# The three changes of stage of a two-layer transformer step: written order on every engine, and twelve modulation chunks in three bursts

## The chip, the core and the metric

One core of a Trainium2 chip runs the whole step. The metric is the device time of one execution in microseconds (us), the median of several runs; smaller is better. TensorE (PE) multiplies, VectorE (DVE) and ScalarE (ACT) do elementwise work, GpSimd (POOL) takes powers, and SyncE's queue (SP) issues nearly all transfers (DMA).

## What is computed

Two rows of tokens, stream 0 (128 context tokens) and stream 1 (128 latent tokens), go through two layers of width 2048 with the same weights, in fp32:

```
sh_a, sc_a, gt_a, sh_m, sc_m, gt_m = silu(c) @ w_ada + b_ada      # modulation, per layer and per stream
h = rms_norm(x, g1) * (1 + sc_a) + sh_a                           # pre-norm
x = x + gt_a * rms_norm(attention(h @ w_in) @ w_out, g2)          # attention half
h = rms_norm(x, g3) * (1 + sc_m) + sh_m
x = x + gt_m * rms_norm(relu(h @ w_up)**2 @ w_down, g4)           # MLP half, width 8192
```

## The kernel before

**Products.** A weight chunk is 1 MB: 128 rows of 2048 numbers, which hold two k-tiles (128 inputs each) for 1024 outputs. `issue` (line 1003) loads chunks on SP's queue, in one order for the whole kernel, into five buffers (`NRAW`); a buffer is filled again when its chunk is used. `split_to` (1012) splits each half chunk (one k-tile) into a high part `wh` (an ACT copy, 1020) and a low part `wl` (a DVE subtraction, 1021), three pairs deep (`NW`). `Group.run` (350) multiplies: per k-tile, stream and 512 outputs three products, `xh*wh`, `xh*wl` and `xl*wh` (365 to 367), so 24 products a chunk. The left sides lie transposed and split in `XT[0..3]`, four k-tiles each.

**A change of stage** lies between the last product of one half layer and the first product of the next. There are three: attention to MLP in layer 0, MLP of layer 0 to attention of layer 1, and attention to MLP in layer 1. At each, for both streams, the last outputs are squared for the norm (864 or 937) and multiplied by the gate rows (865 or 938). `residual` (316) then adds them to x (326) and squares the new x (330); `rstd` (104) takes the root on POOL (107). `make_xt` (261) scales x by it (269 for stream 0 on DVE, 271 for stream 1 on ACT), transposes blocks of 128 columns on PE (`tr`, line 120), applies scale and shift (280 on DVE, 282 on ACT), and splits into XT (287 on ACT, 288 on DVE).

**Modulation.** A column block of 512 of `w_ada` is either four chunks on PE (`ada_mm`, 139: eight products of 32 columns of the array each; then a copy `pt`, 151, transposes and small sums in `ada_post`, 158), or four chunks of the transposed weights on DVE (`dv_mul`, 206: two passes over the chunk, line 212, with `sB`, silu of c, as the other factor). `PE_BLOCKS` and `DV_BLOCKS` say which block goes where. PE chunks are woven between the product chunks, the DVE chunks of layer 1 run under the MLP of layer 0. At each change of stage PE has eight chunks: four from the chunk buffers (`TAIL`, or the first four of `last`) and four that `ahead` (722) loaded early into the then idle XT tiles. They all run right behind the last product of the old stage.

**Order.** A planner places each engine's instructions by the order in which they are written and by when its own model has them ready; it may move one ahead of others. `behind` (109) pins single ones. Transfers are moved too: at the second change the reload of `sB` (204) and the store of x (309) are written some chunks into the new stage.

Of the kernel before, what the change touches and what calls it, by code (L numbers as in the profile page):

```python
# [19 lines left out]
L = 2  # L20
D = 2048
# [9 lines left out]
TAIL = 4  # L31
# [6 lines left out]
DV_BLOCKS = [G_M, M_A + M_M[:4] + G_A[:3] + G_M]  # L38
PE_BLOCKS = [M_A[2:] + G_A + M_M, M_M[4:] + G_A[3:]]
# [28 lines left out]
def trunk(ctx: ExitStack, tc: tile.TileContext, I, O):  # L68
    nc = tc.nc
    pe, act, dve, pool = nc.tensor, nc.scalar, nc.vector, nc.gpsimd  # L70
# [45 lines left out]

    mark = {"pt": None, "res": None, "xt": None}

# [20 lines left out]
    def ada_mm(l, blks, t, kq, raw, half=None):  # L139

        w = 512 if half is None else 256
        if (t, kq) == (0, 0):
            ada_live["ps"] = ps.tile([P, 512], F32, tag="ada", bufs=1, name="ada")
        pa = ada_live["ps"]
        end = t == len(blks) - 1 and kq == 3
        for g in range(4):
            pe.matmul(pa[32 * g:32 * g + 32, 0:w], sT[:, 4 * kq + g, 2 - 2 * t:34 - 2 * t], raw[:, g * w:(g + 1) * w],  # L147
                      start=((t, kq) == (0, 0)), stop=end, tile_position=(0, 32 * g))
        if end:
            pt = sb([P, 512], "pt")  # L150
            mark["pt"] = act.activation(pt[:, 0:w], pa[:, 0:w], AF.Copy)
            fast.append(ada_post(l, blks, pt, 0 if half is None else 2 * half, w // P))
# [104 lines left out]
    def new_xt():  # L257
        for f in range(4):
            XT[f] = sb([P, 4, 2, 256], f"XT{f}", dt=F32R)

    def make_xt(l, w, f, j0=0, j1=4):

        scl, sh = mods[l][2 * w], mods[l][2 * w + 1]
        c, cn = slice(512 * f + P * j0, 512 * f + P * j1), slice(P * j0, P * j1)
        for s in range(2):
            r = xr[s][:, s:s + 1]
            xn, t = nt[0][:, 2 * s], nt[0][:, 2 * s + 1]
            if s == 0:
                dve.tensor_scalar(xn[:, cn], x[s][:, c], r, None, ALU.mult)
            else:  # L270
                act.activation(xn[:, cn], x[s][:, c], AF.Copy, scale=r)
            m = psm()
            for j in range(j0, j1):
                tr(m[:, j * P:(j + 1) * P], xn[:, j * P:(j + 1) * P])
            step = 2 if f == 0 else 4
            for j in range(j0, j1):
                k = 4 * f + j
                jc = slice(j * P, (j + 1) * P)
                if s == 0:
                    dve.tensor_scalar(t[:, jc], m[:, jc], scl[:, k, s:s + 1], sh[:, k, s:s + 1], ALU.mult, ALU.add)  # L280
                else:
                    act.activation(t[:, jc], m[:, jc], AF.Identity, bias=sh[:, k, s:s + 1], scale=scl[:, k, s:s + 1])
                if (j + 1) % step == 0:
                    i = j + 1 - step
                    tv = t[:, i * P:(j + 1) * P].rearrange("p (j q) -> p j q", j=step)
                    hi = XT[f][:, i:j + 1, 0, s * P:(s + 1) * P]
                    act.activation(hi, tv, AF.Copy)  # L287
                    lo = dve.tensor_tensor(XT[f][:, i:j + 1, 1, s * P:(s + 1) * P], tv, hi.bitcast(F32), ALU.subtract)
        mark["xt"] = lo
# [26 lines left out]
    def residual(rows, ss, last, s):  # L316

        if not last and s == 0:
            nt[0] = sb([P, 4, 512], "big", 5)
        r = st2()  # L320
        dve.tensor_reduce(r[:, 0:1], ss[:, s, :], AX.X, ALU.add)
        rstd(r[:, 0:1], r[:, 0:1], D, 1)
        ss2 = st2()
        for n in range(4):
            c = slice(n * 512, (n + 1) * 512)
            u = dve.scalar_tensor_tensor(x[s][:, c], rows[s][:, c], r[:, 0:1], x[s][:, c], ALU.mult, ALU.add)  # L326
            if last:
                nc.sync.dma_start(O["yp" if s == 0 else "ys"][:, c], x[s][:, c])
            else:
                q = act.activation(rows[s][:, c], x[s][:, c], AF.Square, accum_out=ss2[:, n:n + 1])  # L330
                if s == 1 and n == 2:
                    behind(q, mark["pt"])
        if s == 0:
            mark["res"] = u
        if not last:
            xr[s] = st2()
            dve.tensor_reduce(xr[s][:, s:s + 1], ss2[:, 0:4], AX.X, ALU.add)
            rstd(xr[s][:, s:s + 1], xr[s][:, s:s + 1], D, 1)


    class Group:


        def __init__(self, ntile, nk, lhs, done, seg=None):
# [3 lines left out]
            self.q = self.cnt = 0  # L348

        def run(self, steps):  # L350

            if self.acc is None:
                self.acc = [[ps.tile([P, 512], F32, tag="acc", bufs=NACC, name="acc") for _ in range(self.n)]
                            for _ in range(2)]
            q, i0 = self.q, self.cnt - self.segs[self.q]
            seg = self.segs[q + 1] - self.segs[q]
            end = i0 + len(steps) == seg
            for s in range(2):
                for n in range(self.n):
                    a = self.acc[s][n]  # L360
                    for i, (kt, wh, wl) in enumerate(steps):
                        first, last = i0 + i == 0, i0 + i == seg - 1
                        c = slice(n * 512, (n + 1) * 512)
                        xh, xl = self.lhs(kt, s, 0), self.lhs(kt, s, 1)
                        pe.matmul(a, xh, wh[:, c], start=first, stop=False)  # L365
                        pe.matmul(a, xh, wl[:, c], start=False, stop=False)  # L366
                        pe.matmul(a, xl, wh[:, c], start=False, stop=last)  # L367
                    if end:
                        self.done(s, n, a, q)
# [352 lines left out]
    def ahead(ada):  # L722
# [9 lines left out]
        def use():  # L732
            for t, it in zip(held, ada):
                ada_mm(*it[2], t)
                step_list(fast, 1)
# [28 lines left out]
    for l in range(L):  # L764
# [34 lines left out]
        call(new_xt)  # L799
        call(begin)  # L800
# [34 lines left out]
        else:  # L835
            for f in range(4):
                call(lambda f=f: make_xt(1, 0, f))
            cG[0].insert(3, ("call", store_x))
            cG[0].insert(1, ("call", reload_sb))
# [19 lines left out]
        def wout_done(nh, S=S, l=l):  # L859
            def f(s, n, a, _):  # L860
# [4 lines left out]
                dve.tensor_tensor(S["rows"][s][:, c], S["rows"][s][:, c], a, ALU.mult)  # L865
                if (nt, s) == (1, 1):
                    load_x()
                if (nt, s) == (3, 0):
                    residual(S["rows"], ssA[0], False, 0)
# [5 lines left out]
        for nh in range(2):  # L875
            rest += tchunks(I["w_out"][l], 8 * nh, 8, Group(2, KT, o_lhs(), wout_done(nh)), ko, need)
# [7 lines left out]
        weave(rest[cut:], fill[nf:], tail=TAIL)  # L884

        def after_attn(S=S, l=l, use=use):
            mark["tail"] = mark["pt"]
            use()
            drain_dv()
            drain_fast()  # L890
            new_xt()
            mark["pt"] = mark["tail"]
            residual(S["rows"], ssA[0], False, 1)

        call(after_attn)
        for f in range(4):
            call(lambda f=f, l=l: make_xt(l, 1, f))
# [25 lines left out]
        def down_done(q, nh, M=M, l=l):  # L923
            def f(s, n, a, _):
# [9 lines left out]
                if q == 3:  # L934
# [3 lines left out]
                    dve.tensor_tensor(rw[:, c], rw[:, c], sB[s][:, c], ALU.mult)  # L938
                    if (nt, s) == (3, 0):
                        residual(M["rows"], ssA[1], l == L - 1, 0)  # L940
            return f

        if l + 1 < L:
            last = ada_items(1, G_A[3:] + M_M[4:5])
            load, use = ahead(last[4:])
        rest = []
        for q in range(4):
            for g in range(2 * q, 2 * q + 2):
                rest += tchunks(I["w_up"][l], 8 * g, 8, Group(2, KT, xl, up_done(g)), k2)
            for nh in range(2):  # L950
                al = lambda kt, s, p, M=M, q=q: M["a"][4 * q + kt // 4][:, kt % 4, p, s * P:(s + 1) * P]
                rest += tchunks(I["w_down"][l], 16 * q + 8 * nh, 8, Group(2, KT, al, down_done(q, nh)), k2)
            if q == 3 and l + 1 < L:
                rest.insert(-8, ("call", load))
        if l + 1 < L:
            rest.insert(1, ("call", load_sb))
            g, m = dv_items(0, G_M), dv_items(1, M_A + M_M[:4])
            dv = [x for i in range(16) for x in m[3 * i:3 * i + 3] + g[i:i + 1]]
            weave(rest[:4], [])
            weave(rest[4:115], [], dv)  # L960
            call(lambda: (drain_dv(), drain_fast()))
            items.append(rest[115])
            call(lambda l=l: load_gates(l, 1, sB, slice(0, D)))
            call(lambda l=l: layer_consts(l + 1))
            items.extend(rest[116:])
            items.extend(last[:4])
        else:
            weave(rest[:2], [])
            weave(rest[2:100], [], dv_items(1, G_M))
            call(lambda: (drain_dv(), drain_fast()))  # L970
            items.append(rest[100])
            call(lambda l=l: load_gates(l, 1, sB, slice(0, D)))
            items.extend(rest[101:])

        def after_mlp(M=M, l=l, use=use):
            if l + 1 < L:
                mark["tail"] = mark["pt"]
                use()
                mark["pt"] = mark["tail"]
            drain_fast()  # L980
            residual(M["rows"], ssA[1], l == L - 1, 1)

        call(after_mlp)
# [10 lines left out]
    chunks = [it for it in items if it[0] != "call"]  # L994
# [17 lines left out]
    def split_to(k):  # L1012
        while state["split"] <= min(k, len(subs) - 1):
            i, j = subs[state["split"]]
            if i not in raws:
                return
            r = raws[i][:, j * 1024:(j + 1) * 1024]
# [3 lines left out]
            behind(dve.tensor_tensor(wl, r, wh.bitcast(F32), ALU.subtract), mark["res"])  # L1021
# [128 lines left out]
```

## Time and profile before

| | us |
|---|---|
| runs: median of 3 (lowest, highest) | 2297.96 (2296.06, 2302.87) |
| the profiled execution, its own time | 2295.36 |
| its span in the profile | 2293.3 |
| PE busy | 2223.2 (97%) |
| DVE busy | 1592.6 (69%) |
| ACT busy | 1072.2 (47%) |
| mean granted TensorE clock | 0.993 of full |

How to read it: the span runs from the first to the last instruction. The line of an instruction is that of `kernel.py`; all transposes have line 120. A wait is written "engine line <- what released it". The granted clock is a share of 2.4 GHz. PE is busy nearly all of the time, so the time ends with PE's work and the gaps in it.

### The profile page before, as it was taken

The numbers are of one execution on the slowest core, as the hardware profiler recorded it, in microseconds if no ns is written. First come the engines' busy times: TensorE is split into PE (matmuls) and PEld (weight loads), VectorE is DVE, ScalarE is ACT, GpSimd is POOL, SyncE is SP. The second block draws the span as 40 slices with busy tenths as digits, with TensorE's granted clock in tenths as the row PEclk, the third lists the DMA queues.
The fourth block names the chain that finished last, engine by engine and source line by source line (L and its number), as shares of the span: only waits on it lengthen the run. The fifth ranks groups of instructions, "written<-read, shape, count | busy, mean of one in ns | idle before, by whom it ended". The sixth has DMA issues, their size and how long they took to land.

```text
span 2293.3 us, 26818 instructions
## 1 busy us (share of the span) xinstructions
PE 2223.2 (97%) x10460; PEld 1746.8 (76%) x10460; DVE 1592.6 (69%) x1967; ACT 1072.2 (47%) x1483; POOL 23.3 (1%) x30
## 2 busy tenths in 40 slices
PE   6999999999999999999999999999999999999997
PEld 3667666678888888888867777876888888888886
DVE  2566745499899998999668787548566566565445
ACT  4334444365445434434446455545544543443443
POOL 0000000000000000000000000000000000000000
PEclk9999999999999999999999999999999999999999
DMA  8888787978788887788868666766566566556652
GB/s 335 313 336 333 300 313 309 397 295 298 295 310 300 298 302 294 282 295 313 317 225 299 237 248 218 270 232 230 205 230 233 203 220 236 205 211 223 221 189 93
DMA packets 94539, 611.40 MB, mean 267 GB/s; under 512 B 14026, under 2 KB 16458, under 8 KB 22730
## 3 DMA queue, kind: packets, MB, share of 16 engines
q1 hardware_dynamic: 93836, 609.21, 72.1%
q8 instruction: 82, 1.34, 0.2%
q10 hardware_dynamic: 576, 0.48, 0.1%
q14 instruction: 45, 0.37, 0.0%
HBM read 601.97 MB, written 7.68 MB: 266 GB/s over the span
## 4 chain that ended last, share of the span: by engine, by line
PE 82%; DVE 7%; DMA 4%; ACT 3%; issue 2%; POOL 1%; SPq 0%; POOLq 0%; DVEq 0%; ACTq 0%
PE acc L366 25%; PE acc L367 25%; PE acc L365 25%; DVE wl L1021 3%; PE m L120 3%; PE ada L147 2%; DMA raw<-w_adaT_in 2%; ACT wh L1020 1%; ACT qT L918 1%; DMA raw<-w_in_in 1%; POOL st L107 1%; DMA raw<-w_ada_in 1%; DVE junk L212 1%; PE m L456 1%; DVE stg L326 0%
## 5 line engine op out<-in xcount | busy, mean ns | idle before, releaser
L1020 ACT ACTIVATE wh<-raw 128x1024 fp32r<-128x1024 f32 x720 | 759.2, 1060 | 961.1 <-PE acc L367 862.2
L1021 DVE TENSOR_TENSOR wl<-raw,wh 128x1024 fp32r<-128x1024 f32 x720 | 873.4, 1222 | 471.5 <-ACT wh L1020 469.7
L365 PE MATMUL acc<-wh,XT 128*128 128x512 f32 x1600 | 629.0, 399 | 10.8 <-ACT XT L287 5.9
L366 PE MATMUL acc<-wl,XT 128*128 128x512 f32 x1600 | 629.5, 394 | 4.9 <-DVE wl L1021 4.6
L367 PE MATMUL acc<-wh,XT 128*128 128x512 f32 x1600 | 625.9, 392 | 0.0
L366 PE MATMUL acc<-wl,big 128*128 128x512 f32 x1280 | 500.8, 391 | 1.3 <-DVE wl L1021 1.1
L365 PE MATMUL acc<-wh,big 128*128 128x512 f32 x1280 | 498.3, 393 | 0.6 <-ACT wh L1020 0.3
L367 PE MATMUL acc<-wh,big 128*128 128x512 f32 x1280 | 498.1, 390 | 0.0
L365 PEld LDWEIGHTS acc<-wh,XT 128*128 128x128 f32 x1600 | 301.3, 189 | 91.1 <-ACT wh L1020 14.1
L366 PEld LDWEIGHTS acc<-wl,XT 128*128 128x128 f32 x1600 | 301.9, 189 | 74.0 <-DVE wl L1021 13.4
L367 PEld LDWEIGHTS acc<-wh,XT 128*128 128x128 f32 x1600 | 301.7, 189 | 61.9
L365 PEld LDWEIGHTS acc<-wh,big 128*128 128x128 f32 x1280 | 239.9, 188 | 59.7 <-issue 5.0
L366 PEld LDWEIGHTS acc<-wl,big 128*128 128x128 f32 x1280 | 240.4, 188 | 53.3 <-DVE wl L1021 4.5
L367 PEld LDWEIGHTS acc<-wh,big 128*128 128x128 f32 x1280 | 240.4, 188 | 49.7
L212 DVE SCALAR_TENSOR_TENSOR junk<-raw,sB 128x2048 fp8e5<-128x2048 f32 x92 | 210.4, 2286 | 13.5 <-DMA raw<-w_adaT_in 13.0
L212 DVE SCALAR_TENSOR_TENSOR raw<-raw,sB 128x2048 f32<-128x2048 f32 x92 | 210.1, 2284 | 0.1
L147 PE MATMUL ada<-raw,sT 128*32 128x512 f32 (+1 forms) x768 | 95.0, 574 | 15.2 <-DMA raw<-w_ada_in 15.1
L147 PEld LDWEIGHTS ada<-raw,sT 128*32 128x32 f32 x768 | 20.8, 110 | 60.1 <-issue 36.6
L911 DVE TENSOR_TENSOR big<-tmp,big 128x512 fp32r<-128x512 f32 x64 | 43.8, 687 | 30.1 <-ACT big L910 29.8
L775 DVE TENSOR_TENSOR stg<-stg,acc 128x512 f32<-128x512 f32 x64 | 42.8, 684 | 27.6 <-PE acc L367 27.4
L918 ACT ACTIVATE qT<-acc 128x512 f32<-128x512 f32 x64 | 37.9, 594 | 18.9 <-PE acc L367 17.9
L107 POOL TENSOR_TENSOR st<-st,hf 128x1 f32<-128x1 f32 (+2 forms) x26 | 23.1, 894 | 2263.7 <-DVE st L106 2068.9
(123 smaller groups left out, 919.2 us busy)
## 6 DMA issues: line engine op xcount, KB each, us to landing
raw<-w_up_in SPq DMA_DIRECT2D x128, 1024.0 KB, 5.3
raw<-w_down_in SPq DMA_DIRECT2D x128, 1024.0 KB, 4.9
raw<-w_adaT_in SPq DMA_DIRECT2D x92, 1024.0 KB, 4.9
raw<-w_ada_in SPq DMA_DIRECT2D x80, 1024.0 KB, 7.3
raw<-w_in_in SPq DMA_DIRECT2D x72, 1024.0 KB, 6.4
raw<-w_out_in SPq DMA_DIRECT2D x32, 1024.0 KB, 6.2
XT<-w_ada_in SPq DMA_DIRECT2D x12, 1024.0 KB, 7.8
raw<-w_ada_in SPq DMA_DIRECT2D x16, 512.0 KB, 5.0
```

The source lines that it names most:

```text
L107: pool.tensor_tensor(out, out, hf[:, 0:width], ALU.pow)
L120: pe.transpose(out, in_, ident)
L147: pe.matmul(pa[32 * g:32 * g + 32, 0:w], sT[:, 4 * kq + g, 2 - 2 * t:34 - 2 * t], raw[:, g * w:(g + 1) * w], start=((t, kq) == (0, 0)), st ...
L212: p = dve.scalar_tensor_tensor(o, raw, 1.0, sB[v], ALU.mult, ALU.mult, accum_out=a[:, j, v:v + 1], saturate=None if v else False)
L365: pe.matmul(a, xh, wh[:, c], start=first, stop=False)
L366: pe.matmul(a, xh, wl[:, c], start=False, stop=False)
L367: pe.matmul(a, xl, wh[:, c], start=False, stop=last)
L775: dve.tensor_tensor(o, o, a, ALU.add)
L911: dve.tensor_tensor(A[:, :, 1, s * P:(s + 1) * P], uv, hi.bitcast(F32), ALU.subtract)
L918: act.activation(t, a, AF.Relu)
L1020: act.activation(wh, r, AF.Copy)
L1021: behind(dve.tensor_tensor(wl, r, wh.bitcast(F32), ALU.subtract), mark["res"])
```

## The change

It marks every instruction on PE, ACT, DVE and POOL, from the products of a stage's last chunk on, to stay in written order on its engine (`keep`), and writes each change of stage out by hand (`edge_run`); `keep(False)` ends the marks. Transfers are not marked. `TAIL` is 8 instead of 4, so twelve modulation chunks stand at each change: four held in XT, eight in the buffers. In the attention halves the four more were woven earlier. At the second change they are the block `M_M[3]` of layer 1, which goes from DVE to PE. The copy `pt` of the sums comes at the end (`ada_end`); sums of two blocks that are opened there use one of the three `m` banks. The weight splits of the new stage begin inside. The reload of `sB`, the store of x and the last two quarters of XT are written behind it.

```diff
-TAIL = 4
+TAIL = 8
-DV_BLOCKS = [G_M, M_A + M_M[:4] + G_A[:3] + G_M]
-PE_BLOCKS = [M_A[2:] + G_A + M_M, M_M[4:] + G_A[3:]]
+DV_BLOCKS = [G_M, M_A + M_M[:3] + G_A[:3] + G_M]
+PE_BLOCKS = [M_A[2:] + G_A + M_M, M_M[3:] + G_A[3:]]
+            def g(*a, **k):
+                i = f(*a, **k)
+                if mark["keep"]:
+                    tc.keep_in_program_order(i)
+                return i
...
+    def edge_done(rows, ss, s, n, last, mul):
+
+        if (n, s) == (2, 0):
+            edge["mul"] = mul
+        elif (n, s) == (3, 0):
+            edge["mul"]()
+            edge["r0"] = res_scale(ss, 0)
+            mul()
+        elif (n, s) == (2, 1):
+            edge["ss2"] = res_add(rows, edge["r0"], 0, last)
+            edge["mul"] = mul
+        elif (n, s) == (3, 1):
+            edge["mul"]()
+            if not last:
+                nt[0] = sb([P, 4, 512], "big", 5)
+                res_norm(0, edge["ss2"])
+            edge["r1"] = res_scale(ss, 1)
+            mul()
+            edge["rows"] = rows
+        else:
+            mul()
+
+    def edge_run(l, w, held, g, ada, part, weights):
+
+
+        held(0, 1)
+        for i in range(4):
+            ada(i)
+        held(1, 3)
+        ada(4)
+        new_xt([0])
+        m = xt_turn(0, 0, 0, 2)
+        ada(5)
+        part(0, True, True)
+        part(1, True, False)
+        xt_fin(l, w, 0, 0, m, 0, 2)
+        g.open()
+        g.piece(0, 0, weights(0))
+        m = xt_turn(0, 0, 2, 4)
+        ss2 = res_add(edge["rows"], edge["r1"], 1, False)
+        part(1, False, True)
+        res_norm(1, ss2)
+        held(3, 4)
+        ada(6)
+        ada(7)
+        g.piece(0, 1, weights(1))
+        new_xt([1, 2, 3])
+        m1 = xt_turn(0, 1, 0, 2)
+        xt_fin(l, w, 0, 1, m1, 0, 2)
+        xt_fin(l, w, 0, 0, m, 2, 4)
+        g.piece(1, 0, weights(0))
+        m = xt_turn(0, 1, 2, 4)
+        xt_fin(l, w, 0, 1, m, 2, 4)
+        part(2, True, True)
+        m = xt_turn(1, 0, 0, 4)
+        g.piece(1, 1, weights(1))
+        g.cnt += 2
+        ada_end()
+        xt_fin(l, w, 1, 0, m, 0, 4)
+        keep(False)
+        xt_fin(l, w, 1, 1, xt_turn(1, 1, 0, 4), 0, 4)
...
+            if whole and g.final:
+                split_to(k0 + 1)
+                keep(True)
```

In it `held(a, b)` multiplies the chunks held in XT and `ada(i)` one from the buffers. `xt_turn(f, s, j0, j1)` scales columns j0 to j1 of quarter f of stream s and transposes them; `xt_fin` applies scale and shift and splits into XT. `part(k, hi, lo)` makes `wh` and `wl` of half chunk k of the new stage, `g.piece(s, i, ...)` runs the six products of stream s with half chunk i. `res_scale`, `res_add` and `res_norm` are the three parts of `residual`.

## Rows read from the trace of the kernel before

**Rows 1.** The page's part 1, busy time of each engine.

```profile
PE 2223.2 (97%) x10460; PEld 1746.8 (76%) x10460; DVE 1592.6 (69%) x1967; ACT 1072.2 (47%) x1483; POOL 23.3 (1%) x30
```

**Rows 2.** Windows, PE, at three changes: length, busy, clock, DMA share, GB/s.

```profile
452.70:474.00 21.30, 16.10 (x122) 1.00 1.00 405
1191.20:1212.50 21.30, 14.96 (x98) 0.84 0.92 368
1547.30:1568.60 21.30, 15.72 (x105) 0.84 0.62 247
```

**Rows 3.** Waits of PE, whole span: total us, times, longest.

```profile
PE m L120 <- ACT pt L151: 10.4, 9, 2.6
PE acc L365 <- ACT XT L287: 5.9, 2, 4.7
PE m L120 <- ACT big L271: 3.0, 1, 3.0
```

**Rows 4.** Windows, PE, where the clock was low (columns as in rows 2).

```profile
1204.00:1210.50 6.50, 4.58 (x15) 0.50 1.02 393
...
1559.00:1565.50 6.50, 4.38 (x15) 0.50 0.56 237
```

**Rows 5.** Timeline, first change, PE: start, us, engine, line, what.

```profile
457.03 0.66 PE L120 MATMUL m<-cs,pt 128*128 128x128 f32 x4 [2.40 <-ACT pt L151]
...
461.69 3.62 PE L147 MATMUL ada<-XT,sT 128*32 128x512 f32 x32
```

**Rows 6.** Timeline, end of the MLP of layer 0, PE; 48 products apart.

```profile
1176.17 0.39 PE L365 MATMUL acc<-wh,big 128*128 128x512 f32 x1
...
1187.05 0.39 PE L365 MATMUL acc<-wh,big 128*128 128x512 f32 x1
```

**Rows 7.** Timeline, first change, DVE, POOL and ACT.

```profile
453.00 2.73 DVE L326 SCALAR_TENSOR_TENSOR stg<-stg,st 128x512 f32<-128x512 f32 x4
...
462.75 0.55 POOL L107 TENSOR_TENSOR st<-st,hf 128x1 f32<-128x1 f32 x1 [4.62 <-DVE st L106]
...
467.11 1.06 ACT L1020 ACTIVATE wh<-raw 128x1024 fp32r<-128x1024 f32 x1 [0.69 <-DMA raw<-w_up_in]
...
468.08 0.79 ACT L282 ACTIVATE big<-m,mod,mod 128x128 f32<-128x128 f32 x2
...
468.69 0.72 DVE L280 TENSOR_SCALAR big<-m,mod,mod 128x128 f32<-128x128 f32 x2
...
469.72 0.41 ACT L287 ACTIVATE XT<-big 128x256 fp32r<-128x256 f32 x1
470.00 0.48 DVE L269 TENSOR_SCALAR big<-stg,st 128x512 f32<-128x512 f32 x1
...
470.37 0.73 ACT L271 ACTIVATE big<-stg,st 128x512 f32<-128x512 f32 x1
470.40 0.42 DVE L288 TENSOR_TENSOR XT<-big,XT 128x256 fp32r<-128x256 f32 x1
...
470.73 1.22 DVE L1021 TENSOR_TENSOR wl<-raw,wh 128x1024 fp32r<-128x1024 f32 x1
```

**Rows 8.** The page's part 6: transfers of 1 MB, us from issue to landing.

```profile
raw<-w_adaT_in SPq DMA_DIRECT2D x92, 1024.0 KB, 4.9
raw<-w_ada_in SPq DMA_DIRECT2D x80, 1024.0 KB, 7.3
```

**Rows 9.** Timeline of SP's queue at the second change.

```profile
1191.29 0.33 SPq L204 DMA_DIRECT2D sB<-silu  x1
...
1199.14 0.70 SPq L309 DMA_DIRECT2D xd<-stg  x1
```

**Rows 10.** Windows in the MLPs of layers 0 and 1: PE, PEld, DVE, ACT, POOL.

```profile
500.00:1146.00 646.00, 643.58 (x2881) 526.98 (x2880) 579.31 (x586) 297.68 (x338) 0.00 (x0) 1.00 0.82 301
1700.00:2270.00 570.00, 569.56 (x2552) 469.32 (x2551) 329.77 (x311) 260.75 (x292) 0.00 (x0) 1.00 0.59 209
```

**Rows 11.** The page's part 5: one of the two DVE passes over a chunk.

```profile
L212 DVE SCALAR_TENSOR_TENSOR raw<-raw,sB 128x2048 f32<-128x2048 f32 x92 | 210.1, 2284 | 0.1
```

More of the change, by code (lines that the diff above doesn't have):

```diff
@@ L255, in trunk, with new_xt, xt_turn @@
     nt = [None]
-    def new_xt():
-        for f in range(4):
+    def new_xt(fs=range(4)):
+        for f in fs:
             XT[f] = sb([P, 4, 2, 256], f"XT{f}", dt=F32R)
+    def xt_turn(f, s, j0, j1):
+        c, cn = slice(512 * f + P * j0, 512 * f + P * j1), slice(P * j0, P * j1)
+        r = xr[s][:, s:s + 1]
+        xn = nt[0][:, 2 * s]
+        if s == 0:
+            dve.tensor_scalar(xn[:, cn], x[s][:, c], r, None, ALU.mult)
+        else:
+            act.activation(xn[:, cn], x[s][:, c], AF.Copy, scale=r)
+        m = psm()
+        for j in range(j0, j1):
+            tr(m[:, j * P:(j + 1) * P], xn[:, j * P:(j + 1) * P])
+        return m
@@ L314, in load_x, with res_scale @@
             nc.sync.dma_start(x[s], xd[s])
-    def residual(rows, ss, last, s):
-        if not last and s == 0:
-            nt[0] = sb([P, 4, 512], "big", 5)
+    def res_scale(ss, s):
         r = st2()
@@ L322, in residual, with res_add @@
         rstd(r[:, 0:1], r[:, 0:1], D, 1)
+        return r
+    def res_add(rows, r, s, last):
         ss2 = st2()
@@ L329, in residual @@
             else:
[L330 to L338, printed above, removed]
+                act.activation(rows[s][:, c], x[s][:, c], AF.Square, accum_out=ss2[:, n:n + 1])
@@ L341, in trunk, with edge_items @@
+    def edge_items(l, w, tail, held, first):
+        items.append(("edge", tail[:4] + [first] + tail[4:], (l, w, held)))
     class Group:
@@ L348, in __init__, with open, piece @@
             self.q = self.cnt = 0
+            self.final = False
+        def open(self):
+            self.acc = [[ps.tile([P, 512], F32, tag="acc", bufs=NACC, name="acc") for _ in range(self.n)]
+                        for _ in range(2)]
+        def piece(self, s, i0, steps, n0=0, n1=None):
+            seg = self.segs[self.q + 1] - self.segs[self.q]
+            for n in range(self.n)[n0:n1]:
+                a = self.acc[s][n]
+                for i, (kt, wh, wl) in enumerate(steps):
+                    c = slice(n * 512, (n + 1) * 512)
+                    xh, xl = self.lhs(kt, s, 0), self.lhs(kt, s, 1)
+                    pe.matmul(a, xh, wh[:, c], start=(i0 + i == 0), stop=False)
+                    pe.matmul(a, xh, wl[:, c], start=False, stop=False)
+                    pe.matmul(a, xl, wh[:, c], start=False, stop=(i0 + i == seg - 1))
         def run(self, steps):
             if self.acc is None:
[L353 to L357, printed above, removed]
+                self.open()
+            i0 = self.cnt - self.segs[self.q]
+            end = self.left() == len(steps)
             for s in range(2):
                 for n in range(self.n):
[L360 to L367, printed above, removed]
+                    self.piece(s, i0, steps, n, n + 1)
                     if end:
-                        self.done(s, n, a, q)
+                        self.done(s, n, self.acc[s][n], self.q)
             self.cnt += len(steps)
@@ L730, in load, with use @@
                 held.append(t)
-        def use():
-            for t, it in zip(held, ada):
+        def use(a, b):
+            for t, it in list(zip(held, ada))[a:b]:
                 ada_mm(*it[2], t)
-                step_list(fast, 1)
         return load, use
@@ L883, in trunk @@
             weave(rest[:cut], fill[:nf], dv)
[L884 to L897, printed above, removed]
+        weave(rest[cut:-1], fill[nf:-TAIL])
+        call(lambda: (drain_dv(), drain_fast()))
+        items.append(rest[-1])
+        end_attn = fill[-TAIL:], use
         M = {"a": [None] * 16}
@@ L970, in trunk @@
+            end_mlp = last[:8], use
+        else:
+            weave(rest[:4], [])
+            weave(rest[4:102], [], dv_items(1, G_M))
             call(lambda: (drain_dv(), drain_fast()))
-            items.append(rest[100])
+            items.append(rest[102])
             call(lambda l=l: load_gates(l, 1, sB, slice(0, D)))
[L973 to L981, printed above, removed]
@@ L983, in trunk @@
-        call(after_mlp)
+            items.extend(rest[103:])
+            call(lambda M=M: (res_add(M["rows"], edge["r1"], 1, True), keep(False)))
     def drain_dv():
@@ L991, in drain_fast @@
             step_list(fast, 1)
-    chunks = [it for it in items if it[0] != "call"]
+    chunks = [c for it in items if it[0] != "call" for c in (it[1] if it[0] == "edge" else [it])]
     raws = {}
@@ L1027, in split_to @@
                 issue()
+        return True
+    def split_to(k):
+        while state["split"] <= min(k, len(subs) - 1):
+            if not split_part(state["split"], True, True):
+                return
     ci = 0
```

185 lines of the change are left out of this document (116 added, 69 removed).

## The prediction

> **What bounds the kernel now.** I read the busy times first: PE works for 2223.2 of 2293.3 us [rows 1], and in the MLPs it has next to no gap, 2.4 us in 646 and 0.4 in 570 [rows 10]. So the time is PE's work plus its stands, and the change can win only stands. Then I took the windows at the three changes of stage. In stretches of 21.3 us PE is busy for 16.1, 15.0 and 15.7 [rows 2]: stands of 5.2, 6.3 and 5.6. The waits say on what: the copy `pt` of the modulation sums, the first XT, the scaled x of stream 1 [rows 3]. At the second and third change the granted clock also lay at 0.50 (1.2 of 2.4 GHz) for some 6.5 us, in which PE worked 4.58 and 4.38 [rows 4]; at full clock that is half, so another 2.3 and 2.2. At the first change it stayed at 1.00. The three changes thus lose 5.2 + 8.6 + 7.8 = **21.6 us**, and that is all there is to win there.
>
> **The new change of stage, by hand.** Zero is the end of the old stage's last product. A modulation chunk takes 3.62 / 4 = 0.905 us [rows 5]. A product takes 0.227 (10.88 us for 48) [rows 6], so a piece of six takes 1.36. Two transposes take about 0.35, half of 0.66 [rows 5] and a little.
>
> *First burst.* One held chunk, four from the buffers, two held: PE is full until 6.3. Meanwhile stream 0's chain runs: root 0.55, four additions 2.73 [rows 7], squares, root again, scaling. From the output that ends at -2.7 this comes to about 5 us, in the MLP to 6.4 with its extra additions. The transposes come only after the eighth chunk, so the chain is covered, and the waits for `pt` [rows 3] are gone, since the copy now comes last.
>
> *Transfers.* The eighth chunk's buffer is free when the first buffered chunk is multiplied, at 1.8. On an empty queue 1 MB lands after 4.9 [rows 8], at 6.7: PE stands 0.4. The next ones follow at the rate of the transfers, 405 GB/s [rows 2], one per 2.6 us: 9.3, 11.9, 14.5. PE wants the ninth at 8.0 (stand 1.3), reaches 10.2, runs piece (0, 0), two transposes, a held chunk and the next one until 13.7, and stands 0.8 for the last. Together **2.5**. With the median of all PE chunks, 7.3 [rows 8], it would be 4.9; with transfers that never pace, 0. I take 2.5, since the edge starts with full buffers and few transfers outstanding. The Trainium skill's page "DMA: Bandwidth & Descriptors" (Bandwidth, Measured) gives 6.15 us for 1 MB from another queue; by that figure the first stand would be 1.3 longer, and the trace's 4.9 decides.
>
> *Behind the last burst* (15.4) there is no modulation left to cover anything. Piece (0, 1) and stream 1's first transposes end at 17.1. Now PE waits for two affine steps on ACT (0.79) and the high part (0.41) [rows 7]: with handovers **1.3**. Piece (1, 0) runs for 1.36. Its next transposes need scaled x from ACT, and ACT must first make the high part of stream 0's other half, for which DVE must first end stream 1's low part (0.42) and two affine steps (0.72); then 0.41 and about half of 0.73 [rows 7], some 2.2 in all: a stand of **0.8**. Then comes the long one. Written between stream 1's second transposes and those of quarter 1 is the split of the next half chunk. On ACT: 0.79, 0.41, `wh` 1.06. DVE's `wl` (1.22) waits for that, and the scaling of quarter 1 (0.48) [rows 7] is written behind `wl`; PE's transposes wait for the scaling, and piece (1, 1), which has all it needs, is written behind the transposes. 3.96 and five handovers of 0.05: **4.2 us** in which PE has nothing marked to do. Unmarked products of the second chunk need the same `wl`, so at most the last 0.5 of it can be filled.
>
> So 6.3 + 2.5 = 8.8 per change, 26.4 for three. At the second, SP's queue took the reload of `sB` as soon as the old stage was done with it, and the store of x soon after [rows 9]. Both will again be free between 0 and 6. None ahead of the chunks costs 0, two cost up to 3 (5.2 less what PE does not wait for). I take half, 1.5: **27.9**.
>
> *The clock.* Before, it fell at the changes where the longest stands were 4.7 and 3.0, not where it was 2.4 [rows 3, 4]. The new stand of 4.2 follows 3.7 us of which 2.1 are stands, so it is nearer to the first two. I take it as falling at all three, for 2.2 each [rows 4]: **6.6**; the bounds are 0 and 3.3 each, half of 6.5. The Trainium skill's page "TensorE: Matmul & The Clock Gate" (HAM oscillation) says that bursts of products parted by long waits each start at the lower clock. By it all three fall; the first change, which kept 1.00, speaks against; by that row alone the sum would be 6.6 lower.
>
> **The other parts.** The block that goes from DVE to PE adds 4 x 0.905 = **+3.6** on PE, with the same bytes. It takes 4 x 2 x 2.284 = 18.3 us from DVE [rows 11], which is busy for 579 of 646 in that MLP; PE's gap there is 2.4 against 0.4 in 570 where DVE has half the load [rows 10], so between -2.0 and 0: **-1.0**. The four chunks that were woven earlier in the attention halves cost PE the same in either place: 0, with up to +1.8 in layer 1, where two of them stood near attention's own waits. No split of a new-stage weight now runs ahead of the change; both first ones fit into ACT's and DVE's free time before 9. The modulation sums hold one of three `m` banks longer; two are left and the transposes use two: 0. At the kernel's end the marks leave DVE's order as it is: 0, within 1 either way. What is late next is quarter 1 for stream 1, scaled on ACT behind the stand; PE then has the second chunk's 24 products (5.4 us), which cover it.
>
> **Sum.** 27.9 + 6.6 - 21.6 + 3.6 - 1.0 = +15.5 on the profiled execution's 2295.36: **2311**. Its time lies 2.6 below the median of the runs shown, inside their spread. A measurement of this kernel can tell 0.3% (6.9 us) from no change.
>
> **Rivals.**
> *The clock stays at 1.00* at all three, as at the first change before: 6.6 less, 2304. It decides at the long stand. For: products run densely for 17 us before it. Against: rows 3 and 4 together. 0.22.
> *The order is not held at the long stand*, and so not slower: if the planner lets DVE scale quarter 1 before `wl`, PE's transposes follow at once, the 4.2 are gone and the clock has no cause to fall: 3 x 4.2 + 6.6 = 19.2 less, 2292. It decides with the place of that scaling (0.48) among DVE's instructions. For: the planner moves much today, as the reload in rows 9. Against: all instructions concerned are marked. 0.13.
> *Transfers pace harder*: chunks land after 7.3 instead of 4.9, so 2.4 more a change: 2318. For: that is the median of such chunks, and the second change's queue is crowded. Against: the buffers are full at zero. 0.15.
> My forecast has 0.50.
>
> **Range and chances.** The forecast's own range is 2304 to 2317 (clock partly falling, 0 to 3 at the second change, -2.0 to 0 from DVE). To hold 0.8 it must take in the clock's rival and most of the third: 2294 to 2319. Faster by over 0.3% (under 2291) is half of the second rival and a little: 0.09. Slower (over 2305) is the forecast nearly whole, the third rival and a third of the first: 0.66. The rest, 0.25, is within.
>
> **What would show it.** In the new trace: no wait of PE for `pt` at the changes; waits for modulation transfers of 0.4 to 1.3; some 20 us after the old stage's end a stand of about 4 us before four transposes, released by DVE's scaling (line of `xt_turn`), with `wh` and `wl` just before it; a clock of 0.50 behind it. It is wrong if that stand is missing, if PE's busy share in the 27 us behind a change is over 0.85, or if losses shrink elsewhere, say in the MLP of layer 0, by more than 2.

## The result and the profile after

The changed kernel takes 2311.17 us (median of 5 runs, 2307.83 to 2312.38), the kernel before 2297.96 (5 runs): a ratio of 1.0057, 95% interval 1.0043 to 1.0071, so 10 to 16 us slower. The profiled execution took 2311.17 with a span of 2309.2, 15.9 longer than before's span; between the medians the difference is 13.2. The forecast was 2311: 15.5 more than before's profiled execution, which lay 2.6 under the median. The sum was met; not all of its terms were, and the experiments show which.

The page's part 1 of the changed kernel, against [rows 1]:

```profile
PE 2238.5 (97%) x10496; PEld 1749.8 (76%) x10496; DVE 1577.3 (68%) x1955; ACT 1073.8 (47%) x1487; POOL 25.5 (1%) x30
```

PE works 15.3 us more. Its 36 further instructions (32 products and 4 transposes of the moved block) explain some 4 of that. DVE works 15.3 less. Span less busy time is 70.7 us, before 70.1: over the whole kernel PE stands hardly longer, and its busy time grows by nearly as much as the span. A lower clock makes products longer, and that counts as busy: summed as below over the whole span it costs 14.7 us, before 8.6. So stands and clock must be read together, and stage by stage.

Windows of the changed kernel, PE: length, busy, clock, DMA share, GB/s. First the 28 us from the end of the old stage's last product at each change, then the stretches in which the clock was low.

```profile
450.40:478.40 28.00, 20.05 (x132) 0.97 0.93 382
1198.87:1226.87 28.00, 20.42 (x126) 0.89 0.98 406
1555.44:1583.44 28.00, 20.48 (x131) 0.92 0.83 338
476.86:480.07 3.21, 3.21 (x11) 0.50 0.24 59
...
1210.59:1214.00 3.41, 3.41 (x16) 0.50 1.01 428
...
1224.62:1231.03 6.41, 5.94 (x16) 0.50 0.78 291
1579.60:1586.03 6.43, 5.52 (x14) 0.50 0.53 190
```

Stands of 8.0, 7.6 and 7.5 us answer to the 5.2, 6.3 and 5.6 of before. The clock falls at all three changes, at the second even twice; busy time times (1 - clock) gives 1.6, 1.7 + 3.0 and 2.8, so 9.1 in all, against 4.7 before.

Waits of PE in the changed kernel (whole span: us in total, times, longest), against [rows 3]. All compute lines read L82, the line of the new wrapper, so one goes by tiles. `m<-raw` is a modulation product whose sums lie in an `m` bank.

```profile
PE acc L82 <- ACT wh L82: 13.1, 6, 3.0
...
PE m L82 <- DMA raw<-w_ada_in: 9.2, 8, 2.4
PE acc L82 <- DVE wl L82: 6.0, 8, 2.0
PE acc L82 <- ACT XT L82: 4.0, 3, 1.3
...
PE m L82 <- ACT big L82: 0.9, 3, 0.3
```

No wait for `pt` is left at a change. In its place stand transfers of modulation chunks (9.2 us, eight waits), the first XT of stream 1 (three times 1.3), its scaled x (three times 0.3) and, once per change, 2.8 us for `wh`. The timeline shows that last one at the first change (start, us, engine, line, what; in brackets the idle time before it and what ended it):

```profile
470.16 0.50 PE L82 MATMUL acc<-wh,XT 128*128 128x512 f32 x1 [1.34 <-ACT XT L82]
...
472.11 0.44 PE L82 MATMUL m<-cs,big 128*128 128x128 f32 x2 [0.28 <-ACT big L82]
475.31 0.73 PE L82 MATMUL acc<-wh,XT 128*128 128x512 f32 x2 [2.76 <-ACT wh L82]
476.57 0.68 PE L82 MATMUL acc<-wl,XT 128*128 128x512 f32 x1 [0.53 <-DVE wl L82]
...
477.47 1.05 PE L82 MATMUL m<-cs,big 128*128 128x128 f32 x4
...
472.59 0.81 ACT L82 ACTIVATE big<-m,mod,mod 128x128 f32<-128x128 f32 x2 [0.53 <-PE m L82]
473.29 0.72 ACT L82 ACTIVATE big<-stg,st 128x512 f32<-128x512 f32 x1
473.90 0.41 ACT L82 ACTIVATE XT<-big 128x256 fp32r<-128x256 f32 x1
474.20 1.05 ACT L82 ACTIVATE wh<-raw 128x1024 fp32r<-128x1024 f32 x1
...
475.29 1.23 DVE L82 TENSOR_TENSOR wl<-raw,wh 128x1024 fp32r<-128x1024 f32 x1 [0.52 <-ACT wh L82]
476.43 0.48 DVE L82 TENSOR_SCALAR big<-stg,st 128x512 f32<-128x512 f32 x1
```

This is the forecast chain, instruction by instruction: affine steps, high part, `wh`, `wl`, DVE's scaling of quarter 1, and only then four transposes. Two things were not forecast. The planner put unmarked products of the second chunk into PE's stand, so `wh` ends it and not the scaling. And it put an unmarked scaling of stream 1 (473.29, 0.72 us) between ACT's marked steps, which makes the same stand longer.

Outside the changes the first MLP lost more than before. Windows and timeline there, changed kernel:

```profile
1070.00:1080.00 10.00, 8.02 (x29) 0.83 0.56 193
500.00:1146.00 646.00, 642.34 (x2872) 1.00 0.81 295
```

```profile
1064.90 1.06 ACT L82 ACTIVATE wh<-raw 128x1024 fp32r<-128x1024 f32 x1 [0.16 <-PE acc L82]
...
1068.43 2.29 DVE L82 SCALAR_TENSOR_TENSOR junk<-raw,sB 128x2048 fp8e5<-128x2048 f32 x1 [2.44 <-DMA raw<-w_adaT_in]
...
1070.65 0.69 DVE L82 TENSOR_TENSOR big<-tmp,big 128x512 fp32r<-128x512 f32 x1
1071.25 2.35 DVE L82 TENSOR_TENSOR wl<-raw,wh 128x1024 fp32r<-128x1024 f32 x2
...
1072.52 0.50 PE L82 MATMUL acc<-wl,XT 128*128 128x512 f32 x1 [1.98 <-DVE wl L82]
```

DVE waits 2.44 us for a modulation chunk, multiplies it, does one more step, and only then makes the `wl` that PE stands for, though the `wh` for it, counted in order, is the one that was there at 1065.96. The Trainium skill's page "PSUM — Partial Sum Buffer" (Engine vs sequencer instructions) says that DVE's queue is strictly first in, first out; these rows agree. So less work on DVE (566 us of 646, before 579 [rows 10]) does not mean fewer stands for PE: what counts is which transfer stands ahead of a split.

### The profile page after: what moved, and what is told of

It is laid out like the page before. It is cut to its first block, busy times and chain, and to the rows that moved or that the text cites. A ratio compares the mean times of both kernels' runs of the same rounds, so it can differ in the third digit from the quotient of the medians.

```text
span 2309.2 us, 26881 instructions
## 1 busy us (share of the span) xinstructions
PE 2238.5 (97%) x10496; PEld 1749.8 (76%) x10496; DVE 1577.3 (68%) x1955; ACT 1073.8 (47%) x1487; POOL 25.5 (1%) x30
## 3 DMA queue, kind: packets, MB, share of 16 engines
q8 instruction: 82, 1.34, 0.2%
## 4 chain that ended last, share of the span: by engine, by line
PE 82%; DVE 6%; DMA 6%; ACT 3%; issue 3%; POOL 0%; SPq 0%; POOLq 0%; DVEq 0%; ACTq 0%
PE acc L82 74%; PE m L82 5%; DVE wl L82 3%; PE ada L82 3%; DMA raw<-w_ada_in 2%; DMA raw<-w_adaT_in 2%; ACT wh L82 1%; DVE junk L82 1%; DVE stg L82 1%; DMA raw<-w_in_in 1%; ACT qT L82 1%; DVE raw L82 1%; POOL st L82 0%; ACT big L82 0%; ACT tmp L82 0%
## 5 line engine op out<-in xcount | busy, mean ns | idle before, releaser
L82 ACT ACTIVATE wh<-raw 128x1024 fp32r<-128x1024 f32 x720 | 759.1, 1060 | 964.6 <-PE acc L82 862.2
L82 DVE TENSOR_TENSOR wl<-raw,wh 128x1024 fp32r<-128x1024 f32 x720 | 874.7, 1223 | 480.9 <-ACT wh L82 479.4
L82 PE MATMUL acc<-wh,XT 128*128 128x512 f32 x3200 | 1030.0, 397 | 17.2 <-ACT wh L82 13.1
L82 PE MATMUL acc<-wh,big 128*128 128x512 f32 x2560 | 800.3, 391 | 0.0
L82 PEld LDWEIGHTS acc<-wh,XT 128*128 128x128 f32 x3200 | 604.2, 190 | 164.2 <-ACT wh L82 23.0
L82 PE MATMUL acc<-wl,XT 128*128 128x512 f32 x1600 | 632.1, 395 | 5.8 <-DVE wl L82 5.2
L82 PEld LDWEIGHTS acc<-wh,big 128*128 128x128 f32 x2560 | 480.3, 188 | 107.4 <-issue 4.0
L82 PE MATMUL acc<-wl,big 128*128 128x512 f32 x1280 | 500.5, 391 | 0.9 <-DVE wl L82 0.8
L82 PEld LDWEIGHTS acc<-wl,XT 128*128 128x128 f32 x1600 | 303.0, 189 | 75.8 <-DVE wl L82 15.3
L82 PEld LDWEIGHTS acc<-wl,big 128*128 128x128 f32 x1280 | 240.4, 188 | 52.0 <-DVE wl L82 3.9
L82 DVE SCALAR_TENSOR_TENSOR junk<-raw,sB 128x2048 fp8e5<-128x2048 f32 x88 | 201.3, 2287 | 17.1 <-DMA raw<-w_adaT_in 16.5
L82 DVE SCALAR_TENSOR_TENSOR raw<-raw,sB 128x2048 f32<-128x2048 f32 x88 | 201.1, 2286 | 0.1
L82 DVE TENSOR_TENSOR stg<-stg,acc 128x512 f32<-128x512 f32 x128 | 85.3, 684 | 46.5 <-PE acc L82 38.3
L82 PE MATMUL ada<-raw,sT 128*32 128x512 f32 (+1 forms) x704 | 90.6, 580 | 15.1 <-DVE st L82 10.9
L82 PEld LDWEIGHTS ada<-raw,sT 128*32 128x32 f32 x704 | 19.8, 111 | 59.5 <-issue 34.1
L82 DVE TENSOR_TENSOR big<-tmp,big 128x512 fp32r<-128x512 f32 x64 | 43.7, 688 | 28.1 <-ACT big L82 28.1
L82 DVE TENSOR_REDUCE st<-m 128x2 f32<-128x512 f32 (+3 forms) x45 | 23.1, 528 | 48.8 <-PE m L82 48.6
L82 POOL TENSOR_TENSOR st<-st,hf 128x1 f32<-128x1 f32 (+2 forms) x26 | 25.3, 976 | 2277.5 <-DVE st L82 2194.8
L82 ACT ACTIVATE stg<-acc 128x512 f32<-128x512 f32 x52 | 30.6, 595 | 35.4 <-PE acc L82 35.1
L82 ACT ACTIVATE qT<-acc 128x512 f32<-128x512 f32 x64 | 37.7, 593 | 18.7 <-PE acc L82 17.8
L82 ACT ACTIVATE tmp<-m 128x512 f32<-128x512 f32 x68 | 40.4, 594 | 8.0 <-PE m L82 8.0
L82 DVE TENSOR_TENSOR XT<-big,XT 128x512 fp32r<-128x512 f32 (+1 forms) x40 | 22.9, 583 | 29.8 <-ACT XT L82 29.7
```

The costliest lines, as they stand in the source:

```text
L82: i = f(*a, **k)
```

## The experiments

This table holds the times of the experiments, and from their profiles the stands at the three changes (36 us from the old stage's last product), what the clock cost there, and stands plus clock in the rest of the first MLP. "Clock" sums busy time times (1 - granted clock) over windows of 2 us. Each profile is one execution. Each ratio is to runs of the kernel before that were made beside it (their medians lie between 2295.67 and 2298.47).

| kernel | median us | ratio to before, 95% | stands at the changes | clock there | first MLP |
|---|---|---|---|---|---|
| before | 2297.96 | | 5.2, 6.3, 5.6 | 4.7 | 2.4 |
| changed | 2311.17 | 1.0043 to 1.0071 | 8.0, 7.6, 7.5 | 9.1 | 5.3 |
| split behind | 2308.12 | 1.0035 to 1.0073 | 6.3, 5.9, 5.8 | 4.6 | 11.1 |
| stream 1 early | 2297.81 | 0.9997 to 1.0019 | 4.0, 4.0, 2.9 | 6.1 | 3.5 |
| block alone | 2307.73 | 1.0032 to 1.0067 | 5.3, 8.3, 6.4 | 3.5 | 7.9 |
| no marks | 2297.57 | 0.9995 to 1.0018 | 8.1, 4.0, 2.9 | 2.9 | 3.5 |
| block, old places | 2305.71 | 1.0025 to 1.0044 | 5.2, 8.7, 6.7 | 5.6 | 4.6 |
| buffers first | 2288.23 | 0.9933 to 0.9967 | 3.4, 4.9, 1.6 | 1.7 | 3.7 |
| buffers first, old places | 2289.79 | 0.9952 to 0.9978 | 3.3, 4.5, 1.6 | 0 | 3.0 |
| no marks, old places | 2300.65 | 1.0002 to 1.0028 | 7.8, 4.0, 2.9 | 3.2 | 1.7 |
| reload later | 2287.60 | 0.9935 to 0.9972 | 3.2, 2.6, 1.6 | 0 | 7.7 |
| only buffers first | 2311.09 | 1.0043 to 1.0081 | 7.6, 8.1, 6.9 | 12.1 | 4.5 |

The theory: the written order makes PE stand behind the last burst, the clock falls behind that, and the moved block costs its products. The rivals: the chunks' transfers pace the change; the block; the planner would do no better.

### The split behind the transposes

```diff
+        g.piece(1, 1, weights(1))
+        m = xt_turn(1, 0, 0, 4)
         part(2, True, True)
-        m = xt_turn(1, 0, 0, 4)
-        g.piece(1, 1, weights(1))
```

> The changed kernel, with the split of the next half chunk written behind the transposes of quarter 1, and piece (1, 1) ahead of them. If the split's place made the long stand, piece (1, 1) fills 1.36 us of it and DVE's scaling no longer waits for wl: the stand of 2.76 + 0.53 becomes about 2.0 in two parts, 1.3 less per change, 3.9 in all. If the clock falls because of that one long stand, it now stays and gives back up to 7 more: 2300. If it falls because of all the stands of the change together (5.9 us would be left), it falls as before: 2307. If transfers of modulation chunks pace the change (rival), nothing moves: 2311.

Windows at its three changes, and one in its first MLP:

```profile
449.20:477.20 28.00, 21.70 (x133) 0.88 0.96 383
1202.63:1230.63 28.00, 22.09 (x142) 0.94 0.98 403
1554.60:1582.60 28.00, 22.21 (x149) 1.00 0.82 338
560.00:580.00 20.00, 12.66 (x55) 0.83 0.39 148
```

Its timeline at the third change, and its waits in the first MLP:

```profile
1579.29 1.09 PE L82 MATMUL m<-cs,big 128*128 128x128 f32 x8 [1.28 <-DVE big L82]
```

```profile
PE acc L82 <- DVE wl L82: 5.8, 3, 4.5
PE acc L82 <- ACT wh L82: 2.6, 1, 2.6
```

The long stand shrank to 1.28 at all three changes: its place in the written order made it, as the theory says. Where the transfers came on time (the third change) the clock then stayed at 1.00. At the first two it fell earlier, behind waits for chunks of 2.8 and 2.2 us, and was back at 1.00 before the short stand. At the changes this run loses 22.5 us against 32.2. But the median fell by 3, not by 10, and the two intervals overlap, so even the 3 aren't shown. At 560 to 580 us, where the first MLP turns from the up to the down projection, PE stands another 7.1 us, and the clock falls there. In the trace both passes of a modulation product (569.09 to 573.7) stand on DVE ahead of the split that PE waits for. Nothing written had changed there. The expected 2300 was missed for that reason, and 2307 came near it for another than the one given.

### Stream 1 early

Stream 0's second half ends before the seventh buffered chunk (`ada(6)`); stream 1 is scaled and transposed ahead of the last one:

```diff
...
         ss2 = res_add(edge["rows"], edge["r1"], 1, False)
-        part(1, False, True)
+        xt_fin(l, w, 0, 0, m, 2, 4)
...
         m1 = xt_turn(0, 1, 0, 2)
+        m = xt_turn(0, 1, 2, 4)
+        ada(7)
         xt_fin(l, w, 0, 1, m1, 0, 2)
...
```

> The changed kernel with the whole end of the written order changed: stream 0's second half is finished before the sixth buffered chunk, both halves of stream 1 are scaled and transposed ahead of the last chunk, piece (0, 1) stands ahead of it too, and the split of the next half chunk comes between stream 1's two halves. If the stands behind the last burst come from the order (theory), they go, and of 7.7 us a change the transfers' first two are left and a remainder, some 2.2 to 3: 14 to 16 less, 2295 to 2297, and 2288 to 2290 if the clock then stays at its upper level. If the transfers pace the change (rival), the time only moves to the wait for the last chunk: 2306 to 2311.

Its windows at the three changes:

```profile
450.08:478.08 28.00, 24.04 (x141) 0.88 0.97 391
1194.48:1222.48 28.00, 24.02 (x142) 0.88 0.98 403
1548.01:1576.01 28.00, 25.14 (x163) 1.00 0.89 370
```

13.4 us less than the changed kernel, with the same chunks and the same transfers. The stands behind the last burst are gone; some 3 us of waits for chunks are left at the first two changes, 1.7 at the third, and only behind the longer ones did the clock fall. So the order costs what the theory says, and the transfers set only the first part of a change. It only comes level with before, though PE stands 6.3 us less at the changes: the block's 3.6 is still in it, and the clock there costs 1.4 more. In all PE is busy for 12.1 us longer than before (2235.3 us), which these explain only in part; no run takes the rest apart.

### The block alone, and DVE's chunks at their old places

In the kernel before, `M_M[3]` goes from DVE to PE, its four chunks ahead of the eight of the second change. In the second run DVE's chunks of the first MLP also keep the places that they had:

```diff
...
-            last = ada_items(1, G_A[3:] + M_M[4:5])
-            load, use = ahead(last[4:])
+            last = ada_items(1, M_M[3:4] + G_A[3:] + M_M[4:5])
+            load, use = ahead(last[8:])
...
-            g, m = dv_items(0, G_M), dv_items(1, M_A + M_M[:4])
+            g, m = dv_items(0, G_M), dv_items(1, M_A + M_M[:3])
...
-            items.extend(last[:4])
+            items.extend(last[:8])
```

```diff
-            g, m = dv_items(0, G_M), dv_items(1, M_A + M_M[:3])
+            g, m = dv_items(0, G_M), dv_items(1, M_A + M_M[:3]) + [None] * 4
...
```

> The kernel before, with only the block of modulation columns moved from DVE to PE, its four chunks ahead of the eight at the second change. Theory: 4 x 0.905 = 3.6 us more on PE; DVE's relief in the first MLP gives back nothing (the changed kernel lost 1.2 more there, not 1.0 less), so 2301 to 2302. If the relief counts, 2300. If the block costs more than its products because four more chunks crowd the transfers of that change, 2304 or more.

> As the run with the block alone, but DVE's remaining chunks keep the places in the first MLP that they had before: where the block's four chunks stood, nothing stands. If that run's extra 8 us came from the new places of DVE's chunks (theory: one of them now stands at the turn from the up to the down projection, where DVE and the transfers wait for each other), only the block's 3.6 us are left: 2299 to 2301. If they came from the four further chunks at the second change or from the block as such (rival), it stays at 2305 to 2308.

The second run's timeline and windows at the second change:

```profile
1201.44 1.09 PE L147 MATMUL ada<-raw,sT 128*32 128x512 f32 x8 [2.03 <-DMA raw<-w_ada_in]
1203.87 1.94 PE L147 MATMUL ada<-raw,sT 128*32 128x512 f32 x8 [1.34 <-DMA raw<-w_ada_in]
1207.18 1.08 PE L147 MATMUL ada<-raw,sT 128*32 128x512 f32 x4 [1.37 <-DMA raw<-w_ada_in]
```

```profile
1192.48:1220.48 28.00, 19.30 (x127) 0.82 0.97 387
1202.40:1212.60 10.20, 7.49 (x40) 0.50 1.01 425
```

Both theories of mine were too low. Alone, the block costs 12 us (7 to 15), and with the old places 9 (6 to 10). That is most of what the changed kernel lost, so the block can't be dropped as a rival by these two runs; the runs with stream 1 early, without marks and with the buffers first have the same block and lose nothing. The trace splits the 9: the second change with the attention behind it grew by 7.2, of which 3.6 are the products. Before, PE waited for no chunk there; with twelve it waits three times, 4.7 us, and the clock lies at 0.50 for some 10 us instead of 6.5 [rows 4]. The first MLP adds 2.1. The places of DVE's chunks are only part of it: the first MLP's loss fell from 7.9 to 4.6 with the old ones, but the two intervals of the time overlap, so that gain isn't shown in the time.

### No marks

```diff
-                if mark["keep"]:
-                    tc.keep_in_program_order(i)
```

> The changed kernel as written, but no instruction is marked to keep its place, so the planner orders the changes of stage itself. If the marks hold PE back (theory: PE has work it may not take), part of the 23 us of stands at the three changes is filled: 2299 to 2306. If the marks are innocent and the work just has to wait for its operands (rival), 2309 to 2313.

Its windows at the second and third change:

```profile
1198.76:1226.76 28.00, 23.98 (x159) 1.00 0.97 399
1552.14:1580.14 28.00, 25.52 (x169) 1.00 0.82 338
```

13.6 us less than the changed kernel: the same writing, ordered by the planner, loses 17.9 us at the changes instead of 32.2. It stands 4.0 and 2.9 us at these two changes, and 8.1 at the first. The time lies a little under the range expected by the theory. With this written order, the marks are what made the change slower. The variant with DVE's old places brought nothing:

> As the run without marks, and with DVE's chunks at the places in the first MLP that they had before. If the places cost 2 us, 2295 to 2296; if they don't, 2297 to 2298. Should it go down by more, the planner's order is the better one of the two with the places mended.

2300.65, above the 2295 to 2298 expected of it, though its first MLP lost only 1.7 in the profile; the intervals of the two runs overlap.

### Buffers first

With stream 1 early, and also the buffered chunks ahead of the held ones and stream 1's additions ahead of stream 0's affine steps:

```diff
-        held(0, 1)
         for i in range(4):
             ada(i)
-        held(1, 3)
+        held(0, 3)
         ada(4)
         new_xt([0])
         m = xt_turn(0, 0, 0, 2)
-        ada(5)
-        part(0, True, True)
+        part(0, True, False)
+        ss2 = res_add(edge["rows"], edge["r1"], 1, False)
+        part(0, False, True)
+        xt_fin(l, w, 0, 0, m, 0, 2)
+        res_norm(1, ss2)
+        held(3, 4)
+        ada(5)
...
```

> As the run with stream 1 early, with two more moves: the four buffered chunks come ahead of the held ones, so that each buffer is free 0.9 us earlier, and stream 1's additions stand ahead of stream 0's affine steps, so that its root is known some 5 us earlier. If the waits for chunks follow from when buffers come free (theory), the 3.1 us of them per change fall to 1 to 2, and the stands of a change to 2 to 2.5: 2292 to 2295. If the rate of the transfers sets them whatever the order (rival), they keep their 3 us and the time stays at 2296 to 2298.

> As the run with the buffers first, and with DVE's chunks at the places in the first MLP that they had before. If the new places cost 2 us there (waits for wl of 4.2 in all with clock, 2.4 before), it is 2 less than that run: 2290 to 2293. If not, the same as that run.

Windows of the first of the two, then the second change of the other:

```profile
450.24:478.24 28.00, 24.61 (x156) 0.94 0.98 404
1192.44:1220.44 28.00, 23.16 (x154) 1.00 0.97 392
1544.96:1572.96 28.00, 26.42 (x173) 1.00 0.90 374
```

```profile
1189.04:1217.04 28.00, 23.48 (x157) 1.00 0.97 394
```

2288.23: 8 to 15 us under the kernel before and 23 under the changed one, with all twelve chunks and the marks. That is more than expected. Waits for chunks fell at the first and third change (2.4 and 0.9), but at the second they are 3.8, so neither bet was right everywhere. The run makes both moves at once, and none makes the second alone, so how its 10 us below "stream 1 early" divide between them is not shown. DVE's old places make no difference that these runs can tell. The next run shows what holds the second change:

```diff
-            nc.sync.dma_start(sB[v], sB_d[v:v + 1, :].to_broadcast([P, D]))
+            behind(nc.sync.dma_start(sB[v], sB_d[v:v + 1, :].to_broadcast([P, D])), mark["xt"])
```

> As the run with the buffers first, with the first reload of sB (1 MB) put behind the chunks of the second change on SP's queue, where it stood ahead of them. At that change PE waited 2.4 and 1.5 us for chunks, at the third, which has no reload, 0.9 in all. If the reload makes the difference (theory), the two waits fall together to about 1 and the time by 2 to 3: 2285 to 2287. If the rate of the transfers before the change sets them (rival), they stay within 0.5 us and the time at 2288 to 2290.

Its window and waits at the second change:

```profile
1194.88:1222.88 28.00, 25.40 (x166) 1.00 0.93 382
```

```profile
PE m L82 <- DMA raw<-w_ada_in: 1.6, 1, 1.6
```

3.8 became 1.6, so 2.2 of it went with the reload ahead of the chunks (one profile of each). The median moved by 0.6 only, inside the intervals: in this profile the first MLP lost 7.7 instead of 3.7.

### Only the buffers first

The changed kernel with the first two moved lines of the diff above and nothing else.

> The changed kernel with one move: the four buffered chunks ahead of the first held one. Each buffer is free 0.9 us earlier. If the transfers pace the whole change (rival of the prediction), the first waits shrink by 0.9 each and the time by 2 to 3: 2308. If the end of the change is set by the chain behind the last burst (theory), the stands there (1.3, 0.3 and 3.3 us) stay as they are and only what the chunks wait less is won, less what stream 1's chain then makes PE wait more: 2308 to 2311, with the long stand of 2.8 before wh still there at all three changes.

Waits of PE at its first change:

```profile
PE m L82 <- DMA raw<-w_ada_in: 3.1, 2, 2.1
PE acc L82 <- ACT wh L82: 2.8, 1, 2.8
PE acc L82 <- ACT XT L82: 1.3, 1, 1.3
```

2311.09, no change: the stands behind the last burst are all there, and the clock fell twice at that change, behind the chunks and behind the long stand. Freeing buffers earlier is worth nothing while the order behind it stays as it was; with that order mended, its own share was not measured.

## Why the prediction was right, and where its steps were not

The span's 15.9 us against the forecast's 15.5, term by term (the clock before was forecast as 2.3 + 2.2; the block's products are counted by [rows 5] in both columns):

| term | forecast | trace |
|---|---|---|
| stands at the changes | 27.9 - 17.1 = 10.8 | 23.1 - 17.1 = 6.0 |
| clock at the changes | 6.6 - 4.5 = 2.1 | 9.1 - 4.7 = 4.4 |
| the block's products | 3.6 | 3.6 |
| first MLP, stands and clock | -1.0 | 5.3 - 2.4 = 2.9 |
| attention of layer 1, stands and clock | 0 | 4.0 - 8.3 = -4.3 |
| rest | 0 | 3.3 |

- **`pt` gone, transfers in its place.** Right. The three waits were forecast as 0.4, 1.3 and 0.8; at the first change they are 0.64, 1.03 and 1.36. Per change 3.1 instead of 2.5. The extra 1.5 for the reload and the store at the second change did not show (3.15 there); a price of the reload, 2.2, showed only with the buffers first (3.8 with it, 1.6 without).
- **The two short stands behind the last burst.** 1.34 for 1.3, and 0.28 for 0.8: the chain to stream 1's second scaling took 1.95 us (470.16 to 472.11) instead of 2.2, and the piece that covers it 1.67 instead of 1.36.
- **The long stand.** The mechanism was right: place, chain, all three changes, and it shrinks to 1.28 when the split is moved. Its size was 3.3 at the first change and 2.8 at the others instead of 4.2. The step "at most the last 0.5 of it can be filled" failed: unmarked products needed `wh` only, and end the stand at `wh`. The marked order itself was held: DVE's scaling stands behind `wl`, so the rival in which it is not held is out.
- **Clock.** It fell at all three, so the rival in which it stays is out. The term was too small mainly because at the second change it also fell behind a wait for a chunk of 2.4 us (1.7 of the 2.5 that are missing); at the other two the waits of 1.4 and less left it at 1.00 until the long stand. The Trainium skill's page "TensorE: Matmul & The Clock Gate" (HAM oscillation), by which each burst behind a long wait starts at the lower clock, agrees with the changed kernel; the later runs bound it, since waits of 2.1 and 1.4 at the second change left the clock at 1.00 (buffers first, old places).
- **The block.** Its products cost 3.6, but in the old order the block cost 9 in all: as much again came at the second change and behind it, where PE now waits for chunks and the clock is low for longer, and 2.1 in the first MLP. In the changed kernel these sit in the changes' own terms, so the sum still holds; as a price of the block the step was wrong.
- **DVE's relief.** This step failed in sign. The forecast held that less DVE work means smaller stands. Every run with the block moved and DVE's chunks at the new places lost 3.5 to 11.1 in that MLP, before 2.4; with the old places 1.7 to 4.6. Where it was looked at, what stands there is a split behind a modulation product on DVE, at 1070 us one that waits for its transfer, and the planner's order decides where.
- **Attention.** The step "cost PE the same in either place: 0" failed. The attention of layer 1 gave back 4.3, where 0 to +1.8 was forecast: 2.6 of stands, and one fall of the clock (1.7) that the changed kernel doesn't have there. All nine kernels whose four chunks left the attention halves stand less in the first one (12.0 to 13.4 us; before and the two runs with the block alone 14.9 to 15.3), and a wait of 1.4 in layer 1 is missing in all nine. Why, no run shows. Two of the four chunks of layer 0 had left it already: in the trace before, ten chunks run behind the last product at the first change, not eight.
- **The rest of 3.3** is some 5.5 more of busy time that neither the block's products nor the clock explains, and some 2.2 less of stands and clock at the kernel's start, in the first attention half and in the last MLP. Switches between chunks, pieces and transposes may be what makes PE busy for longer (a chunk alone takes 1.07 us, in a run of four 0.905 [rows 5]); no run tests it.

So the total was met partly by luck, by errors that cancel: 4.8 too much for the stands and 4.3 not seen in attention stand against 2.3 too little for the clock, 3.9 in the MLP and 3.3 of the rest. One of the prediction's own signs of being wrong came true: losses shrank elsewhere by more than 2, in the attention of layer 1. What was right is the mechanism at the changes: a stand of some 3 us behind the last burst, made by the written order, with the low clock behind it.

## What to carry to other kernels

A written order forbids the planner to fill a stand: before marking, walk every engine's queue through it and ask which instruction waits at its head while work that is ready stands behind it. Here the marks cost 13 us with one order, and with another the marked kernel was 9 us faster than the first writing as the planner orders it (the better order was not run without marks). What paid most was to write stream 1's scaling and transposes ahead of the last chunk, with the moves that go with it: 13 us. Moving a split behind transposes that did not need it took 10 us out of the changes in the profile, but the time hardly moved, since another stage lost 6. In a kernel of 2300 us, an untouched stage that is planned anew can move by 3 to 8 us, as much as the change that one wants to measure, so read where the time went before believing a median.

## What the runs showed of the hardware

At the changes the granted clock fell to 0.50 behind stands of 2 to 3 us, but not behind each of them: it fell behind a wait of 2.44 at the first change of the run with the buffers first and stayed at 1.00 behind 2.35 and 1.47 at its second. The time at 0.50 also differs: 6.5 us before [rows 4], in the changed kernel 3.2 at the first change, 3.4 and 6.4 at the second and 6.4 at the third.

A long stand isn't needed. In the attention of layer 1 the clock fell in the kernel before, too, though PE had stood for only 0.84 us, up to 1419.56, and worked on transposes and small products from there on:

```profile
1418.00:1422.20 4.20, 3.36 (x14) 1.00 0.58 233
1422.21:1425.62 3.41, 3.41 (x9) 0.50 0.90 315
```

Five of the ten experiments' kernels show the same fall there, behind waits of 0.81 to 0.83; it costs 1.7 us in most of them.
